# Keys and values as a paced list behind the queries, stored split weights for the filler, and another bank for the decode rows

## The chip, the core and the metric

The kernel runs on one core of a Trainium2 chip. Its time is the device time of one execution in microseconds; the median of three runs stands for a kernel. The engines are TensorE (PE; PEld is its weight load), VectorE (DVE), ScalarE (ACT), GpSimd (POOL) and SyncE (SP), which issues nearly all DMAs from one queue in program order.

## What is computed

One step of a hybrid decoder layer in fp32: 2048 prompt positions of width 1024, and 8 decode rows with 512 cached positions each in pages of 128.

```python
h = rms_norm(x, g)
q, k, v, fz, za, u, gv, zc = split(h @ w_in)        # 4 x 512, 8 heads, 4 x 512 columns
q, k = rms_norm(q, g_q), rms_norm(k, g_k)           # 8 heads of 64
c = cumsum(log_sigmoid(fz + b_f))                   # forget gates
s = q @ k.T * SCALE + c[t] - c[s]                   # causal
attn = softmax(s) @ v
mix = tril(w_s) @ rms_norm(gv) + b_s                # inside chunks of 128 positions
y = x + concat[attn * silu(za), u * mix * silu(zc)] @ w_out
```

The decode rows go through the same layer with keys, values and gates from the paged cache. The outputs are y, k, v and the log gates for both, and the normalised gv rows of the decode rows.

## The kernel before

**Precision.** Each fp32 matmul of the projections is made from three in a faster format: weights and inputs are split into a high and a low part (`wh`/`wl`, `hh`/`hl`), and hi x hi, lo x hi and hi x lo are added up in one PSUM bank.

**Stage one, 0 to about 590 us.** The input projection runs by units of columns `u`, in the order 3, 0, 1, 2 (tokens x columns of q, k, v and the gates), 4 (gv), 5, 6 (u and zc) and 7 (za). `load_unit` loads a unit's raw weights, scales and splits them, one unit ahead. At the end of each unit `sample_products` does the eight decode rows: 16 matmuls into a bank of the tag "acc", which the token products rotate through, too; ACT and DVE add its two halves (the tile `s`, L386 and L387). Keys and queries go to DRAM as `qk_hi` and `qk_lo`, values as `v_st`. Units 5 to 7 do only half of the prompt (`NCP` = 2 of 4 groups of 512 positions); the other half is left for the filler. Pages of cached keys (`kb`) are loaded and multiplied beside it in u=4 to 6.

**Stage two, about 590 to 1160 us.** Causal attention by units (h, c): a head and 512 query positions, c = 0 to 3, with 4c + 4 steps of 128 keys (`values`). One step is two score matmuls (`sc<-q,k`: the keys' high and low parts in `k1`, the high part and the rows of gates in `k2`), an exp on ACT (`p`), an accumulation on POOL (`acc`, L1014, for the denominators) and value matmuls (`av<-p,vst`) in groups. Before a unit its row maxima have to be known: `maxima` makes the scores transposed (`tp<-k,q`, needs only `k2`), reduces them on DVE (`mn`) and stores a row (`mrow`), which is one row of the queries' tile. The maxima run `AHEAD` of a head ahead of the values.

`load_queries` (L903 to L905) issues four DMAs: two of `qk_hi`, one of `qk_lo`, one of `mrow`. It is called `QLEAD` = 6 steps before a unit's end (at the first step of a unit of four) for the unit after. `load_keys` (`k2`, 512 KB, L860) is called at the start of a head's first unit for the next head, `load_values` (`k1` and `vst`, 1.5 MB) when the maxima of a head are through.

**The filler.** Between these steps the other half of units 5 to 7 (`fl<-hh,fh`) is issued, in a dose for each step (`FILL`; `FILL7` in the last three units). `fill_weights` loads 2 x 256 KB of raw weights, POOL scales them (L787), ACT casts the high part (L789), POOL subtracts for the low part (L790). When the filler is through it loads and splits the output weights (`load_out_weights`, `wo`), and then the first tiles of the output projection serve as filler in the last units. `gate` and `out_inputs` load what the products behind the attention need (`gz`, `ga`, `gr`; `g`, `xy`). Units run (0,0) to (5,3), then (6,0), (6,1), (6,2), (7,0), (6,3), (7,1), (7,2), (7,3).

**Stage three, from about 1140 us.** The output projection, `sc<-wo,am`.

**What sets the order.** TensorE's order is the order of the program. `Pe.clock` adds up estimated nanoseconds of matmuls; `later(ns, fn)` runs `fn` when that clock has gone on by ns, and so places DMAs and the work of other engines. On the chip each engine goes through its list in order and waits for what an instruction needs; a DMA that waits on SP holds up the DMAs behind it.

Of the kernel before, what the change touches and what calls it, by code (L numbers as in the profile page):

```python
# [9 lines left out]
F32 = mybir.dt.float32  # L10
F32R = mybir.dt.float32r
# [33 lines left out]
STLAST = 2500.0  # L45
SLAG = 3000.0
LAG = 6400.0
AVB = 8
# [5 lines left out]
UNITS = [(h, c) for h in range(6) for c in range(4)] + [(6, 0), (6, 1), (6, 2), (7, 0), (6, 3), (7, 1), (7, 2), (7, 3)]  # L54
AHEAD = 0.8
QLEAD = 6
PRE = 1.2
# [21 lines left out]
def hymba_step(ctx, tc, x_prompt, x_sample, cache_k, cache_v, cache_logf, page_table, g_norm, w_in,  # L79
# [39 lines left out]
    def s4(dt=F32, t="s4"):  # L119
        return med.tile([P, D], dt, tag="s4", name=tname(t))  # L120
# [26 lines left out]
    class Pe:  # L147

        clock = 0.0
        waiting = []  # L150
        given = 0
        decode, side, steps = 1e12, 1e12, None
        last = None
# [18 lines left out]
    def pump(all_=False):  # L172
        while Pe.waiting and (all_ or Pe.waiting[0][0] <= Pe.clock):
            give()
        if not all_ and Pe.clock >= Pe.side:
            m = next(mgen)
            mdone[0] += m
            Pe.side = Pe.clock + PACE if mdone[0] < AHEAD * MT else 1e12
        if not all_ and Pe.clock >= Pe.decode:
            Pe.decode = Pe.clock + (next(Pe.steps, None) or 1e12)  # L180

    def mm(out, lhsT, rhs, start, stop, ns):
# [84 lines left out]
    def log_sigmoid(out, z, rows, n, take):  # L267
# [20 lines left out]
        nc.vector.scalar_tensor_tensor(out, z, 0.0, c, op0=ALU.min, op1=ALU.subtract)  # L288

    def load_unit(segs, raws=None, between=None):  # L290

        n = sum(m for _, m in segs)
        out = []
        for k in range(KT):
            if k % 2 == 0:
                hi, lo = (s4(F32R, t)[:, :2 * n].rearrange("p (k f) -> p k f", k=2) for t in ("wh", "wl"))
            raw = (raws[k] if raws else raw2())[:, :n]
# [79 lines left out]

    def sample_products(unit, n, segs):
        po = bank("acc")
        for k in range(KT):  # L380
# [398 lines left out]

    def fill_weights(o, pair=None):  # L780
        hi, lo = (t.rearrange("p (k f) -> p k f", k=KT) for t in pair or (s4(F32R, "fh"), s4(F32R, "fl")))
        got = []

        def halves(half, raw):
            for k in range(4):
                kk = 4 * half + k
                nc.gpsimd.tensor_scalar(raw[:, k], raw[:, k], gT[:, kk:kk + 1], 0.0, op0=ALU.mult, op1=ALU.add)  # L787
            sl = slice(4 * half, 4 * half + 4)
            nc.scalar.copy(hi[:, sl], raw)  # L789
            nc.gpsimd.tensor_tensor(lo[:, sl], raw, hi[:, sl].bitcast(F32), op=ALU.subtract)  # L790
            got.extend((hi[:, k], lo[:, k]) for k in range(4 * half, 4 * half + 4))
        for half in range(2):
            raw = raw2().rearrange("p (k f) -> p k f", k=4)
            nc.sync.dma_start(raw, w[half * 512:(half + 1) * 512, o:o + P].rearrange("(k p) f -> p k f", p=P))
            later(FLAG * (1 + half), lambda half=half, raw=raw: halves(half, raw))
        return got
# [3 lines left out]
    def filler():  # L800
        jobs = [(o + f * P, f) for f in range(4) for o in (OZA, OU, OZC)] if NCP < 4 else []
        nxt = first.pop()
# [22 lines left out]
        for cp in range(NCP, 4):  # L825
            mx = s2(t="mxu")
            yield from u_steps(units[0], 0, f, cp, "fl", mx)
            yield 0
            yield from zc_steps(units[1], 0, f, cp, "fl", mx)
            if cp == 3:  # L830
                break
            yield 0
            while "k1" not in heads.get(NH - 1, {}):
                yield -1
            load_out_weights(0)
# [19 lines left out]

    def load_keys(h):

        k2 = s8(F32R, "k2")
        b = 512 + h * HD
        nc.sync.dma_start(k2[:HD].bitcast(F32), qk_hi[b:b + HD])  # L860
        nc.sync.dma_start(k2[HD:HD + 3].bitcast(F32), kx[h])
        return dict(h=h, k2=k2)

    def load_values(hd):

        k1 = s8(F32R, "k1")
        h = hd["h"]
        b = 512 + h * HD
        nc.sync.dma_start(k1[:HD].bitcast(F32), qk_hi[b:b + HD])
        nc.sync.dma_start(k1[HD:].bitcast(F32), qk_lo[b:b + HD])  # L870
        vst = s4(t="vst").rearrange("p (n e) -> p n e", e=HD)
        nc.sync.dma_start(vst, v_st[h])
        hd.update(k1=k1, vst=vst)

# [111 lines left out]
    def values(at):  # L986
# [3 lines left out]
        for kt in range(4 * c + 4):  # L990
            if kt == max(0, 4 * c + 4 - QLEAD) and at + 1 < len(UNITS):
                qload[UNITS[at + 1]] = load_queries(*UNITS[at + 1])
# [69 lines left out]
    def all_maxima():  # L1062
        for h in range(NH):
            yield from maxima(heads[h])
            if h + 1 < NH:
                load_values(heads[h + 1])

# [116 lines left out]
    with ExitStack() as p1:  # L1184
# [32 lines left out]
        for pos, u in enumerate(order):  # L1217
# [3 lines left out]
            if u <= 4:  # L1221
                for i in range(NT):
# [13 lines left out]
                    if i == NT - 2:  # L1236
                        group.insert(0, sample_products(unit, WID[u], SEGS[u]))
                    if u == 4 and i == KSTART:
# [6 lines left out]
                if u == 3:  # L1245
                    gates()
            else:
                for cp in range(NCP):
                    for f in range(2):
# [7 lines left out]
                        if cp == NCP - 1 and f == 1:  # L1257
                            group.insert(0, sample_products(unit, WID[u], SEGS[u]))
                        together(*group)
                    if u == 7 and cp == 0:  # L1260
                        heads[0] = load_keys(0)
                        load_values(heads[0])
                        fw = s8(F32R, "fw")
                        first.append(fill_weights(OZA, (fw[:, :D], fw[:, D:])))
                        Pe.side = Pe.clock + SSTART
# [83 lines left out]
```

## Time and profile before

| | |
|---|---|
| median of 3 runs | 1339.46 us (1339.31 to 1339.51) |
| profiled execution | 1342.54 us, span 1340.8 us, mean granted clock 0.989 |
| TensorE busy | 1297.8 us, 97% of the span |
| POOL busy | 622.2 us, 46% |
| DVE, ACT busy | 649.7 us (48%), 446.7 us (33%) |
| data moved by DMA | 182.56 MB, mean 136 GB/s |

The profile shows one execution. A row of the timeline gives start, duration, engine, line, operation, tile written and tiles read, and in brackets the idle time ahead of it on its engine with what ended it. The waits are given as engine, tile and line, what was waited for, and then the total in us, the number of waits and the longest. SPq is SP's queue of DMA issues.

### The profile page before, as it was taken

What the parts mean: (1) busy time and instruction counts of PE and PEld (TensorE: products, weight loads), DVE (VectorE), ACT (ScalarE), POOL (GpSimd) and SP (SyncE); (2) the same over time, 40 slices, a digit from 0 to 9 for tenths busy, and PEclk for the clock granted to TensorE, in tenths of its full rate; (3) what the DMA queues carried; (4) which work ended last, traced back from release to release, by engine and by line L of the source; (5) the groups of instructions that cost most, each with busy time, mean ns of one, the idle gap of its engine ahead of it and who ended that gap; (6) DMA issues with size and microseconds to landing.
All of it is one profiled execution on the core that took longest, in us unless ns stands there. A gap on an engine that the chain in (4) does not pass through costs nothing.

```text
span 1340.8 us, 19346 instructions
## 1 busy us (share of the span) xinstructions
PE 1297.8 (97%) x6544; PEld 1008.3 (75%) x6544; DVE 649.7 (48%) x1216; ACT 446.7 (33%) x805; POOL 622.2 (46%) x707
## 2 busy tenths in 40 slices
PE   6999999999999999999999999999999998999998
PEld 5999999999887777866666666656656664688877
DVE  4445654534677544264476353444355675322321
ACT  5542322222222110114454443534454456300100
POOL 3113343423223554416778666686768668600000
PEclk9999999999999999999999999999999998999999
DMA  6644353555213665635253845477374645573321
GB/s 218 188 120 111 87 142 111 156 144 152 60 42 102 178 182 146 178 88 134 64 130 107 198 120 142 133 189 180 87 195 117 179 126 198 156 238 121 102 80 47
DMA packets 170213, 182.56 MB, mean 136 GB/s; under 512 B 39106, under 2 KB 125442, under 8 KB 168554
## 3 DMA queue, kind: packets, MB, share of 16 engines
q1 hardware_dynamic: 166226, 172.55, 46.6%
q10 hardware_dynamic: 3488, 8.39, 1.6%
q8 instruction: 52, 0.85, 0.3%
q0 software_dynamic: 400, 0.38, 0.1%
q14 instruction: 47, 0.39, 0.1%
HBM read 121.14 MB, written 60.15 MB: 135 GB/s over the span
## 4 chain that ended last, share of the span: by engine, by line
PE 85%; DMA 5%; DVE 4%; issue 2%; SPq 1%; ACT 1%; POOL 1%; DVEq 0%; ACTq 0%; POOLq 0%
PE acc L183 35%; PE sc L183 22%; PE fl L183 10%; PE av L183 8%; PE tp L183 5%; PE tp L187 3%; DMA q<-qk_lo 1%; PE pm L183 1%; DMA xp<-in_x_prompt_dram 1%; DVE wl L265 1%; DMA vst<-v_st 1%; DVE mn L943 1%; DMA k<-qk_lo 1%; DVE wo L257 1%; DMA kb<-in_cache_k_dram 0%
## 5 line engine op out<-in xcount | busy, mean ns | idle before, releaser
L1014 POOL TENSOR_TENSOR acc<-acc,p 128x512 f32<-128x512 f32 (+3 forms) x256 | 285.9, 1117 | 60.4 <-ACT p L1005 47.3
L1005 ACT ACTIVATE p<-sc,zero 128x512 f32<-128x512 f32 (+1 forms) x320 | 194.7, 624 | 171.4 <-PE sc L183 163.6
L183 PE MATMUL acc<-wh,hh 128*128 128x384 f32 (+2 forms) x640 | 228.8, 358 | 0.0
L183 PE MATMUL acc<-wl,hh 128*128 128x384 f32 (+2 forms) x640 | 223.0, 348 | 0.6 <-DVE wl L265 0.6
L183 PE MATMUL acc<-wh,hl 128*128 128x384 f32 (+2 forms) x640 | 222.8, 348 | 0.6 <-DVE hl L257 0.6
L183 PE MATMUL sc<-q,k 128*128 128x512 f32 (+7 forms) x640 | 202.2, 396 | 9.7 <-ACT p L1005 2.9
L183 PE MATMUL sc<-wo,am 128*128 128x512 f32 x720 | 164.3, 390 | 0.0
L183 PEld LDWEIGHTS sc<-wo,am 128*128 128x128 f32 x720 | 134.9, 188 | 28.2
L945 DVE TENSOR_REDUCE mn<-tp 128x1 f32<-128x320 f32 (+5 forms) x192 | 118.6, 631 | 65.6 <-PE tp L183 64.4
L183 PEld LDWEIGHTS sc<-q,k 128*128 128x128 f32 (+1 forms) x640 | 119.1, 195 | 29.5 <-issue 7.3
L183 PE MATMUL av<-p,vst 128*64 128x512 f32 (+3 forms) x640 | 135.3, 543 | 0.0
L245 POOL TENSOR_SCALAR sm<-sm 128x6 f32<-128x6 f32 (+3 forms) x84 | 20.2, 241 | 238.4 <-DVE sm L398 171.1
L183 PE MATMUL tp<-k,q 66*128 66x384 f32 (+6 forms) x320 | 121.3, 394 | 7.9 <-DVE mn L943 3.4
L183 PEld LDWEIGHTS acc<-wh,hh 128*128 128x128 f32 x640 | 120.7, 189 | 7.2 <-ACT hh L252 0.2
L183 PEld LDWEIGHTS acc<-wl,hh 128*128 128x128 f32 x640 | 120.9, 189 | 5.9 <-DVE wl L265 1.5
L183 PEld LDWEIGHTS acc<-wh,hl 128*128 128x128 f32 x640 | 120.5, 188 | 6.3 <-DVE hl L257 1.2
L183 PEld LDWEIGHTS av<-p,vst 128*64 128x64 f32 x640 | 47.7, 137 | 67.5 <-issue 57.3
L943 DVE TENSOR_REDUCE mn<-tp 128x1 f32<-128x512 f32 (+7 forms) x128 | 66.9, 562 | 60.7 <-PE tp L183 60.6
L246 POOL TENSOR_TENSOR sm<-sm,mhalf 128x6 f32<-128x6 f32 (+3 forms) x84 | 89.6, 1067 | 6.7
L183 PEld LDWEIGHTS tp<-k,q 66*128 66x128 f32 x320 | 61.1, 192 | 34.0 <-DVE mn L943 6.6
L183 PE MATMUL acc<-hh,wh 128*128 128x512 f32 x192 | 76.2, 397 | 5.1 <-DVE s L387 5.1
L1138 DVE TENSOR_TENSOR xy<-xy,sc 128x512 f32<-128x512 f32 x30 | 20.6, 687 | 117.8 <-PE sc L183 117.8
(212 smaller groups left out, 1957.2 us busy)
## 6 DMA issues: line engine op xcount, KB each, us to landing
raw<-in_w_in_dram SPq DMA_DIRECT2D x40, 256.0 KB
kb<-in_cache_k_dram SPq DMA_DIRECT2D x32, 256.0 KB
k<-qk_hi SPq DMA_DIRECT2D x16, 512.0 KB
q<-qk_hi SPq DMA_DIRECT2D x64, 128.0 KB
vb<-in_cache_v_dram SPq DMA_DIRECT2D x32, 256.0 KB
g<-gm SPq DMA_DIRECT2D x16, 512.0 KB
xy<-in_x_prompt_dram SPq DMA_DIRECT2D x16, 512.0 KB
out_dram<-xy ACTq DMA_DIRECT2D x15, 512.0 KB
```

The costliest lines, as they stand in the source:

```text
L183: Pe.last = nc.tensor.matmul(out, lhsT, rhs, start=start, stop=stop).ins
L187: Pe.last = nc.tensor.transpose(out, in_, idn).ins
L245: nc.gpsimd.tensor_scalar(r, ss, inv_n, EPS, op0=ALU.mult, op1=ALU.add)
L246: nc.gpsimd.tensor_tensor(r, r, mhalf[:rows, :n], op=ALU.pow)
L257: nc.vector.tensor_tensor(lo, src, hi.bitcast(F32), op=ALU.subtract)
L265: nc.vector.scalar_tensor_tensor(lo, src, g, hi.bitcast(F32), op0=ALU.mult, op1=ALU.subtract)
L943: nc.vector.tensor_reduce(part[:, j_ % 4, n_:n_ + 1], sp, axis=AX.X, op=ALU.min)
L945: nc.vector.tensor_reduce(part[:, j % 4, n:n + 1], sp, axis=AX.X, op=ALU.min)
L1005: nc.scalar.activation(p[:, n0:], sp[:, n0:], AF.Exp, bias=zero1, scale=-1.0)
L1014: nc.gpsimd.tensor_tensor(acc[:, n0:], acc[:, n0:], p[:, n0:], op=ALU.add)
L1138: nc.vector.tensor_tensor(xy[:, fs], xy[:, fs], po, op=ALU.add)
```

## The change

- `load_head` replaces `load_keys` and `load_values`: it returns the loads of a head as a list, three pieces for `k2` and seven for `k1` and `vst`, of 256 KB each. The list is put up in the second step of a head's first unit for the next head, which is behind the query loads of that unit; one piece goes out 2500 ns of `Pe.clock` later and then one in 3000. Maxima and values issue what is left when they need it.
- Queries are issued ten steps before a unit's end instead of six if the next unit's maxima row is already stored, and else four steps before.
- `AHEAD` goes from 0.8 to 0.65 of a head, `FILL` from 0.50 to 0.46, with 0.9 in a head's first unit.
- `keep_unit` stores the split weights of units 5, 6 and 7 in DRAM (`ws`, 24 DMAs of 512 KB) 5 to 12.5 us after each of these units starts; `fill_weights` loads them from there, 24 DMAs of 512 KB in place of 24 of 256 KB, and POOL's 120 and ACT's 24 instructions at L787 to L790 are gone.
- The decode rows use a bank of the tag "pm" in all units but u=4.
- The filler waits for all of head 7's pieces before it loads output weights, where it waited for `k1`.

The numbers of TensorE's and DVE's instructions stay. The diff, cut:

```diff
-FILL = 0.50
+FILL = 0.46
+FILL0 = 0.9
-AHEAD = 0.8
-QLEAD = 6
+AHEAD = 0.65
+LSTEP = 3000.0
+LHEAD = 2500.0
+VPARTS = 7
+QLEAD = 10
...
     def pump(all_=False):
...
+        if not all_ and Pe.loads and Pe.clock >= Pe.load_at:
+            load_next()
...
+    def load_next():
+        Pe.loads.pop(0)()
+        Pe.load_at = Pe.clock + LSTEP
...
+    def keep_unit(u):
+        for j, pair in enumerate(list(split_)):
+            def store(j=j, pair=pair):
+                for r in range(2):
+                    nc.sync.dma_start(ws[u, :, r, 2 * j:2 * j + 2], pair[r].bitcast(F32))
+            later(KEEPLAG + j * KEEPSTEP, store)
...
-    def sample_products(unit, n, segs):
-        po = bank("acc")
+    def sample_products(unit, n, segs, tag):
+        po = bank(tag)
...
-    def fill_weights(o, pair=None):
+    def fill_weights(b, pair=None):
...
-                nc.gpsimd.tensor_scalar(raw[:, k], raw[:, k], gT[:, kk:kk + 1], 0.0, op0=ALU.mult, op1=ALU.add)
-            nc.scalar.copy(hi[:, sl], raw)
-            nc.gpsimd.tensor_tensor(lo[:, sl], raw, hi[:, sl].bitcast(F32), op=ALU.subtract)
...
-            nc.sync.dma_start(raw, w[half * 512:(half + 1) * 512, o:o + P].rearrange("(k p) f -> p k f", p=P))
+        for r, t in enumerate((hi, lo)):
+            nc.sync.dma_start(t.bitcast(F32), ws[b // 4, :, r, :, b % 4 * P:(b % 4 + 1) * P])
+        later(FLAG, lambda: got.extend((hi[:, k], lo[:, k]) for k in range(KT)))
...
+        return [lambda: keys(0), rows_of, lambda: keys(1)], [
+            lambda: both(0, 0), lambda: both(0, 1), lambda: vals(0),
+            lambda: both(1, 0), lambda: both(1, 1), lambda: vals(1), lambda: hd.update(all=True)]
...
         for kt in range(4 * c + 4):
-            if kt == max(0, 4 * c + 4 - QLEAD) and at + 1 < len(UNITS):
+            if kt == 1 and c == 0 and h < NH - 1:
+                Pe.loads += chain(*load_head(h + 1))
+                Pe.load_at = Pe.clock + LHEAD
+            if at + 1 < len(UNITS) and UNITS[at + 1] not in qload and kt >= 4 * c + 4 - (
+                    QLEAD if UNITS[at + 1] in shifted else 4):
                 qload[UNITS[at + 1]] = load_queries(*UNITS[at + 1])
...
         for h in range(NH):
+            while h not in heads or "k2" not in heads[h] or h and len(Pe.loads) > VPARTS:
...
+                load_next()
             yield from maxima(heads[h])
-            if h + 1 < NH:
-                load_values(heads[h + 1])
...
-                        group.insert(0, sample_products(unit, WID[u], SEGS[u]))
+                        group.insert(0, sample_products(unit, WID[u], SEGS[u], "acc" if u == 4 else "pm"))
...
     for at, (h, c) in enumerate(UNITS):
-        if c == 0 and h < NH - 1:
-            heads[h + 1] = load_keys(h + 1)
+        while "all" not in heads[h]:
+            load_next()
...
-        dose = FILL if at < len(UNITS) - 3 else FILL7
+        dose = FILL7 if at >= len(UNITS) - 3 else FILL0 if c == 0 else FILL
```

How the order on SP changes at three places. The first is around the queries for unit (2,1), which are loaded during (2,0). Before, `q_1059` was loaded behind raw filler weights and the 512 KB `k_1350` of the next head:

```order
645 L794 DMA raw_7636<-in_w_in_dram 128x4x128
646 L794 DMA raw_7638<-in_w_in_dram 128x4x128
647 L1045 DMA rT<-rows 4x128
648 L860 DMA k_1350_7653<-qk_hi 64x2048
649 L861 DMA k_1350_7653<-kx 3x2048
650 L903 DMA q_1059_6268<-qk_hi 64x512
651 L513 DMA mxu_7640<-mixT 128x512
652 L903 DMA q_1059_6268<-qk_hi 64x512
653 L904 DMA q_1059_6268<-qk_lo 64x512
654 L905 DMA q_1059_6268<-mrow 1x512
```

and with the change (here the tile is `q_1047`, and the key piece that follows is `k_1344`):

```order
678 L1076 DMA rT<-rows 4x128
679 L994 DMA mrow<-rows 4x128
680 L930 DMA q_1047_6242<-qk_hi 64x512 x2
681 L931 DMA q_1047_6242<-qk_lo 64x512
682 L932 DMA q_1047_6242<-mrow 1x512
683 L1127 DMA gz_7580<-zT 128x512
...
687 L811 DMA fh_7639<-ws 128x8x128
688 L811 DMA fl_7640<-ws 128x8x128
689 L539 DMA mxu_7643<-mixT 128x512
690 L1059 DMA aT<-at_7575 64x512
691 L883 DMA k_1344_7656<-qk_hi 64x1024
```

The filler weights and the key piece moved from in front of the queries to behind them.

The second place is SP around the queries for unit (3,3). Before, the gate inputs (`gz`, `ga`, `gr`) and the pages of cached values (`vb`) came after them:

```order
764 L1028 DMA aT<-at_8669 64x512
765 L528 DMA zT<-sz_8734 128x512
766 L903 DMA q_1059_6268<-qk_hi 64x512 x2
767 L904 DMA q_1059_6268<-qk_lo 64x512
768 L905 DMA q_1059_6268<-mrow 1x512
769 L1045 DMA rT<-rows 4x128
770 L1094 DMA gz_8832<-zT 128x512
771 L1095 DMA ga_8831<-aT 128x512
772 L1097 DMA gr_8833<-rT 64x512 x2
```

and with the change (the first and the last of four page loads are shown):

```order
803 L994 DMA mrow<-rows 4x128
804 L1127 DMA gz_8712<-zT 128x512
805 L1128 DMA ga_8711<-aT 128x512
806 L1130 DMA gr_8713<-rT 64x512 x2
807 L897 DMA vst_8726<-v_st 128x512
...
811 L677 DMA vb_8728<-in_cache_v_dram 128x512
...
823 L677 DMA vb_8728<-in_cache_v_dram 128x512
824 L930 DMA q_1047_6242<-qk_hi 64x512 x2
825 L931 DMA q_1047_6242<-qk_lo 64x512
826 L932 DMA q_1047_6242<-mrow 1x512
```

The queries moved behind the gate inputs, half of the values and four page loads.

The third place is SP around the queries of the last unit, (7,3). Before, two pairs of output-projection inputs stood between the query pieces:

```order
1037 L967 DMA mrow<-rows 4x128
1038 L903 DMA q_1059_6268<-qk_hi 64x512 x2
1039 L1115 DMA g_11551<-gm 128x1024
1040 L1116 DMA xy_11552<-in_x_prompt_dram 128x1024
1041 L1115 DMA g_11555<-gm 128x1024
1042 L1116 DMA xy_11556<-in_x_prompt_dram 128x1024
1043 L904 DMA q_1059_6268<-qk_lo 64x512
1044 L905 DMA q_1059_6268<-mrow 1x512
```

and with the change:

```order
1087 L1148 DMA g_11335<-gm 128x1024
1088 L1149 DMA xy_11336<-in_x_prompt_dram 128x1024
1089 L1059 DMA aT<-at_11380 64x512
1090 L1114 DMA raw_11391<-in_w_out_dram 128x512
1091 L994 DMA mrow<-rows 4x128
1092 L1076 DMA rT<-rows 4x128
1093 L930 DMA q_1047_6242<-qk_hi 64x512
1094 L1114 DMA raw_11397<-in_w_out_dram 128x512
1095 L930 DMA q_1047_6242<-qk_hi 64x512
1096 L931 DMA q_1047_6242<-qk_lo 64x512
1097 L932 DMA q_1047_6242<-mrow 1x512
```

The output-projection inputs moved ahead of all query pieces, and one load of output weights now stands between the pieces.

More of the change, by code (lines that the diff above doesn't have):

```diff
@@ L46 @@
 SLAG = 3000.0
+KEEPLAG = 5000.0
+KEEPSTEP = 2500.0
 LAG = 6400.0
@@ L151, in hymba_step @@
         given = 0
+        loads, load_at = [], 0.0
         decode, side, steps = 1e12, 1e12, None
@@ L235, in hymba_step @@
     rT = dr.tile([NH, SEQ], F32, name="rT")
+    ws = dr.tile([3, P, 2, KT, 4 * P], F32, name="ws")
     p_s = dr.tile([DB, D_IN], F32, name="p_s")
@@ L288, in log_sigmoid @@
         nc.vector.scalar_tensor_tensor(out, z, 0.0, c, op0=ALU.min, op1=ALU.subtract)
+    split_ = []
+    def keep_unit(u):
[4 more added lines that the diff above has]
+            later(KEEPLAG + j * KEEPSTEP, store)
     def load_unit(segs, raws=None, between=None):
@@ L293, in load_unit @@
         out = []
+        split_.clear()
         for k in range(KT):
@@ L296, in load_unit @@
                 hi, lo = (s4(F32R, t)[:, :2 * n].rearrange("p (k f) -> p k f", k=2) for t in ("wh", "wl"))
+                split_.append((hi, lo))
             raw = (raws[k] if raws else raw2())[:, :n]
@@ L777, in out_sample @@
         nc.sync.dma_start(ys, xys)
-    def fill_weights(o, pair=None):
+    def fill_weights(b, pair=None):
         hi, lo = (t.rearrange("p (k f) -> p k f", k=KT) for t in pair or (s4(F32R, "fh"), s4(F32R, "fl")))
         got = []
[L784 to L793, printed above, removed]
-            nc.sync.dma_start(raw, w[half * 512:(half + 1) * 512, o:o + P].rearrange("(k p) f -> p k f", p=P))
-            later(FLAG * (1 + half), lambda half=half, raw=raw: halves(half, raw))
+        for r, t in enumerate((hi, lo)):
+            nc.sync.dma_start(t.bitcast(F32), ws[b // 4, :, r, :, b % 4 * P:(b % 4 + 1) * P])
+        later(FLAG, lambda: got.extend((hi[:, k], lo[:, k]) for k in range(KT)))
         return got
@@ L800, in filler @@
     def filler():
-        jobs = [(o + f * P, f) for f in range(4) for o in (OZA, OU, OZC)] if NCP < 4 else []
+        jobs = [(b, f) for f in range(4) for b in (8 + f, 4 * (f // 2) + f % 2, 4 * (f // 2) + 2 + f % 2)]
         nxt = first.pop()
@@ L832, in filler @@
             yield 0
-            while "k1" not in heads.get(NH - 1, {}):
+            while "all" not in heads.get(NH - 1, {}):
                 yield -1
@@ L854, in fill, with load_head, keys, rows_of @@
             debt[0] -= got
-    def load_keys(h):
-        k2 = s8(F32R, "k2")
+    def load_head(h):
+        hd = heads[h] = dict(h=h)
         b = 512 + h * HD
[L860 to L873, printed above, removed]
+        def keys(a):
+            if a == 0:
+                hd["k2"] = s8(F32R, "k2")
+            cs = slice(a * 1024, (a + 1) * 1024)
+            nc.sync.dma_start(hd["k2"][:HD, cs].bitcast(F32), qk_hi[b:b + HD, cs])
+        def rows_of():
+            nc.sync.dma_start(hd["k2"][HD:HD + 3].bitcast(F32), kx[h])
+        def both(a, r):
+            if (a, r) == (0, 0):
+                hd["k1"] = s8(F32R, "k1")
+            cs = slice(a * 1024, (a + 1) * 1024)
+            nc.sync.dma_start(hd["k1"][r * HD:(r + 1) * HD, cs].bitcast(F32), (qk_lo if r else qk_hi)[b:b + HD, cs])
+        def vals(a):
+            if a == 0:
+                hd["vst"] = s4(t="vst").rearrange("p (n e) -> p n e", e=HD)
+            nc.sync.dma_start(hd["vst"][:, 8 * a:8 * a + 8], v_st[h, :, 8 * a:8 * a + 8])
+        return [lambda: keys(0), rows_of, lambda: keys(1)], [
+            lambda: both(0, 0), lambda: both(0, 1), lambda: vals(0),
+            lambda: both(1, 0), lambda: both(1, 1), lambda: vals(1), lambda: hd.update(all=True)]
     def pieces(nk):
@@ L1063, in all_maxima @@
         for h in range(NH):
+            while h not in heads or "k2" not in heads[h] or h and len(Pe.loads) > VPARTS:
+                if not Pe.loads:
+                    raise RuntimeError(h)
+                load_next()
             yield from maxima(heads[h])
-            if h + 1 < NH:
-                load_values(heads[h + 1])
     wo_hl = {}
@@ L1247, in hymba_step @@
             else:
+                keep_unit(u - 5)
                 for cp in range(NCP):
@@ L1257, in hymba_step @@
                         if cp == NCP - 1 and f == 1:
-                            group.insert(0, sample_products(unit, WID[u], SEGS[u]))
+                            group.insert(0, sample_products(unit, WID[u], SEGS[u], "acc" if u == 4 else "pm"))
                         together(*group)
                     if u == 7 and cp == 0:
-                        heads[0] = load_keys(0)
-                        load_values(heads[0])
+                        for piece in chain(*load_head(0)):
+                            piece()
                         fw = s8(F32R, "fw")
-                        first.append(fill_weights(OZA, (fw[:, :D], fw[:, D:])))
+                        first.append(fill_weights(8, (fw[:, :D], fw[:, D:])))
                         Pe.side = Pe.clock + SSTART
```

## The prediction

> **What bounds the kernel now.** I read the page first, then who waited for whom on TensorE, then ten-microsecond windows around the waits, then the timelines there.
>
> ```profile
> span 1340.8 us, 19346 instructions
> PE 1297.8 (97%) x6544; PEld 1008.3 (75%) x6544; DVE 649.7 (48%) x1216; ACT 446.7 (33%) x805; POOL 622.2 (46%) x707
> ```
>
> TensorE (PE) is busy for 1297.8 of 1340.8 us. The change issues as many matmuls as before, of the same shapes, so at most 43 us is to be had from its idle time, and beside that what the granted clock costs. The waits of TensorE (total, times, longest):
>
> ```profile
> PE acc L183 <- DVE s L387: 5.1, 3, 2.8
> PE tp L183 <- DVE mn L943: 3.4, 6, 1.2
> PE sc L183 <- ACT p L1005: 2.9, 3, 1.8
> PE sc L183 <- DMA q<-qk_hi: 2.4, 1, 2.4
> PE sc L183 <- DMA q<-qk_lo: 2.3, 1, 2.3
> PE sc L183 <- issue: 1.9, 1, 1.9
> PE fl L183 <- DVE sz L499: 1.8, 2, 1.4
> ```
>
> Windows (PE, PEld, DVE, ACT, POOL busy; granted clock; DMA share; GB/s):
>
> ```profile
> 490.00:500.00 10.00, 9.76 (x43) 8.10 (x44) 4.24 (x7) 2.14 (x3) 7.25 (x7) 1.00 0.72 209
> 750.00:760.00 10.00, 7.51 (x30) 5.14 (x27) 3.79 (x8) 2.68 (x6) 4.32 (x8) 0.83 1.00 215
> 900.00:910.00 10.00, 8.06 (x35) 5.59 (x34) 4.12 (x10) 2.95 (x6) 4.21 (x5) 0.83 1.04 232
> 1110.00:1120.00 10.00, 7.51 (x39) 4.00 (x38) 9.16 (x7) 6.98 (x15) 9.69 (x8) 1.00 0.38 119
> 1120.00:1130.00 10.00, 9.39 (x27) 3.96 (x27) 3.05 (x5) 5.38 (x10) 9.45 (x9) 0.66 0.42 113
> 1130.00:1140.00 10.00, 7.67 (x37) 5.02 (x36) 3.91 (x5) 6.88 (x12) 5.81 (x6) 0.90 1.02 377
> ```
>
> At 750 and 900 the clock is 0.83 over ten microseconds: 10 x 0.17 = 1.7 us of work lost after the wait, beside the wait. The timelines show which waits these are. Entering unit (2,1), the queries were issued behind a 512 KB key load:
>
> ```profile
> 743.46 0.45 SPq L860 DMA_DIRECT2D k<-qk_hi  x1
> 744.52 0.45 SPq L903 DMA_DIRECT2D q<-qk_hi  x1
> 747.35 0.45 SPq L904 DMA_DIRECT2D q<-qk_lo  x1
> 754.45 1.08 PE L183 MATMUL sc<-q,k 128*128 128x512 f32 x2 [2.38 <-DMA q<-qk_hi]
> ```
>
> Entering (4,1) they stood behind four page loads and the key load. The wait is named "issue"; but the last query piece (L905) went out only 3.8 us before the matmul that needs it, and I take it for the same wait. Two us later a 128x512 matmul takes 0.63 us; at the full clock it is 0.40, as in the row at 437.65 further down:
>
> ```profile
> 890.11 3.94 SPq L651 DMA_DIRECT2D vb<-in_cache_v_dram  x4
> 900.75 0.44 SPq L905 DMA_DIRECT2D q<-mrow  x1
> 904.51 0.82 PE L183 MATMUL sc<-q,k 128*128 128x512 f32 x2 [1.94 <-issue]
> 906.59 0.63 PE L183 MATMUL fl<-hh,fh 128*128 128x512 f32 x1
> ```
>
> Entering the last unit, (7,3), 2 MB of out-projection inputs were issued between the two parts of the queries:
>
> ```profile
> 1123.94 2.33 SPq L903 DMA_DIRECT2D q<-qk_hi  x2
> 1127.22 0.33 SPq L1115 DMA_DIRECT2D g<-gm  x1
> 1129.02 0.51 SPq L904 DMA_DIRECT2D q<-qk_lo  x1
> 1134.10 0.48 PE L183 MATMUL sc<-q,k 128*128 128x512 f32 x1
> 1136.91 2.56 PE L183 MATMUL sc<-q,k 67*128 67x512 f32 x7 [2.33 <-DMA q<-qk_lo]
> ```
>
> **The change part by part.** The sum is made against the profiled execution, 1342.54 us around its span of 1340.8; it lies 3.1 us (0.23%) above the median of 1339.46, and I take the 3.1 off at the end.
>
> *Decode rows in another bank: -2.3.* The waits on L387 are 5.1 us in three. The longest ends the stage u=4, which keeps its bank:
>
> ```profile
> 437.07 0.50 PE L183 MATMUL acc<-hh,wh 128*128 128x512 f32 x1 [2.79 <-DVE s L387]
> 437.65 0.40 PE L183 MATMUL acc<-hh,wl 128*128 128x512 f32 x1
> 490.24 0.50 PE L183 MATMUL acc<-hh,wh 128*128 128x512 f32 x1 [1.73 <-DVE s L387]
> ```
>
> The "pm" bank is otherwise used only in u=4, so nothing waits for it in u=5 and u=6: 5.1 - 2.8 = 2.3 go, 1.73 of them in the row at 490. Neither window lost clock (490 to 500: 1.00). Bounds -2.3 to 0, if the next accumulator is no earlier free.
>
> *Queries ahead of the keys, entering (2,1): -4.1.* By the order of SP nothing large now stands in front of them; the first key piece is issued after them. 2.38 of waiting and 1.7 of clock; bounds -4.1 to 0.
>
> *Entering (4,1): -3.0.* The key load is gone from in front, but the four page loads stay, and four gate inputs (768 KB) are now ahead of all query pieces, where they stood between them. The queries are issued a little earlier (QLEAD 10 instead of 6 steps, cut to the unit's length). Of 1.94 + 1.7 = 3.6 I take 3.0, nearer to the full gain because 512 KB less are ahead; bounds -3.6 to 0.
>
> *Queries whose lead falls: +6.* Where the row of maxima is not stored yet, the queries now wait until four steps before the unit's end, six before. Six steps measured 10.2 us (1123.94 to 1134.10), so four are an estimated 6.8 us. In front of (1,3) now stand 1.8 MB (both filler weights, 512 KB each, and three pieces of 256 KB), in front of (3,3) 2.05 MB (gate inputs, half the values, four page loads). At the 215 to 232 GB/s of the windows with a full DMA, those and the 384 KB of the queries themselves take 9.7 and 11 us: 2.9 and 4.2 us too long if all is issued at once, nothing if it is issued earlier. Bounds 0 to 2.9 + 4.2 + 2 x 1.7 = 10.5. I take two us for each, and the clock slice in a little over half the cases: 2 x (2 + 1) = 6.
>
> *Entering (7,3): -1.5.* The 2 MB of g and xy are now issued some 12 us before the queries, but the lead falls to four steps and 256 KB of output weights stand between the query pieces. Of 2.33 + 1.7 = 4.0 I take 1.5; bounds -4.0 to +1.5 (the wait one clock slice longer).
>
> *Filler doses and maxima: -1.* POOL is the bound from 1094 on: 9.69 and 9.45 of 10 us busy, one accumulation after the other:
>
> ```profile
> 1095.10 3.65 PE L183 MATMUL av<-p,vst 128*64 128x512 f32 x16
> 1100.57 9.47 POOL L1014 TENSOR_TENSOR acc<-acc,p 128x512 f32<-128x512 f32 x8 [0.79 <-ACT p L1005]
> ```
>
> 9.47 / 8 = 1.18 us for each, while a step without filler needs two score matmuls and two value matmuls of TensorE at 3.65 / 16 = 0.23 us each, 0.9 us. By the order of TensorE the filler now reaches through (6,3), but the out products enter (7,3) after the ninth step instead of the fourth, so about as many steps stand bare as before. TensorE lost 2.5 us idle in 1110 to 1120. Bounds -3 to +3; I take -1, as by my count of the order a few steps fewer are bare.
>
> *Filler weights loaded, not made: -1.* What goes from POOL and ACT:
>
> ```profile
> L787 POOL TENSOR_SCALAR raw<-raw,gT 128x128 f32<-128x128 f32 x96 | 35.6, 389 | 5.0 <-DMA raw<-in_w_in_dram 5.0
> L790 POOL TENSOR_TENSOR fl<-raw,fh 128x512 fp32r<-128x512 f32 x22 | 28.2, 1283 | 7.2 <-ACT fh L789 7.0
> ```
>
> 64 us of POOL and 24 casts of ACT lie beside TensorE's work, so they are worth at most the waits that their crowding causes: those on mn and sz, 3.4 + 1.8 = 5.2. Bounds -5.2 to 0; I take 1. The new loads wait on SP until TensorE has left their buffer, and the queue stands behind them; that is in the +6.
>
> *Storing the weights: +1.* 24 stores of 512 KB go out in u=5, 6 and 7, 4.2 MB each time within some 10 us.
>
> ```profile
> q1 hardware_dynamic: 166226, 172.55, 46.6%
> q10 hardware_dynamic: 3488, 8.39, 1.6%
> 490.00:540.00 50.00, 49.15 (x214) 39.03 (x215) 23.00 (x32) 6.92 (x10) 28.94 (x26) 1.00 0.63 182
> 540.00:590.00 50.00, 49.19 (x224) 38.55 (x223) 14.87 (x27) 7.50 (x13) 12.29 (x17) 1.00 0.39 106
> POOL kb L668 <- DMA kb<-in_cache_k_dram: 24.4, 15, 6.3
> ```
>
> The queue moves 172.55 MB in 46.6% of the span, 276 GB/s, or 391 in q10's large rows: 11 to 15 us of all DMA engines per stage of 50 us that is 39 to 63% busy. It fits over a stage and not in its moment: a load issued behind it comes up to 15 us late. POOL already waits up to 6.3 us for the pages of keys without a wait of TensorE, so I take 1. Bounds 0 to 13.5 (below).
>
> Sum: -2.3 - 4.1 - 3.0 + 6 - 1.5 - 1 - 1 + 1 = -5.9. 1342.5 - 5.9 = 1336.6, less 3.1: 1333.5 us.
>
> [...]
>
> **The rivals.**
>
> *A, the queries are late elsewhere.* (1,3) and (3,3) cost their bound of 10.5 instead of 6, and (7,3) keeps its wait: -5.9 + 4.5 + 1.5 = +0.1, 1339.6 us. For it speaks that page loads take 3.94 us of SP's time for four; against it that much of the 2 MB is issued well before the queries.
>
> *B, the stores take over (slower).* If the 15 us of backlog exceed the lead of the loads of pages and mixing inputs, the DVE and ACT queues stop behind them and TensorE runs out of accumulators. It decides when a load is over some 12 us late (one group of accumulators, estimated from the 50 us of a stage in four groups). Price, as at 437: 2.8 + 1.7 = 4.5 in each of three stages, 13.5 instead of the 1 in the sum: 1333.5 + 12.5 = 1346.0. Against it: POOL's 6.3 us wait did no harm.
>
> *C, no new waits.* The 6 falls to 0 and (7,3) yields all 4.0: -5.9 - 6 - 2.5 = -14.4, 1325.0 us. For it: the loads ahead wait for their own buffers and may be out early.
>
> *D, the queries are as late as before* in (2,1) and (4,1), since other loads fill the place of the keys: -5.9 + 7.1 = +1.2, 1340.7. The order shows no such load before (2,1).
>
> **How the numbers follow.** A measurement of this kernel can tell 0.2%, 2.7 us, from no change: faster is below 1336.8, slower above 1342.1. Forecast 0.45 (1330 to 1337; nearly all faster), C 0.13 (faster), A 0.19 and D 0.06 (nearly all within 0.2%), B 0.17 (slower). Faster 0.57, same 0.24, slower 0.19. The range reaches from C to the middle of B: 1324 to 1345.
>
> **What would show it.** Right: no wait on s at 490 and 538, none entering (2,1), clock 1.00 there; a wait of one to five us on q entering (1,3) or (3,3); POOL some 64 us less busy. Wrong: waits on s or mxu around 500 to 590 (B); q waits in (2,1) (D); a longer bare stretch in (7,2) and (7,3), where POOL's accumulations set the pace and a later out projection costs more than the 3 allowed; or the first filler weights late at 590, behind their own stores.

## The result, and the profile after

The changed kernel took 1326.85 us (median of 5 runs, 1325.52 to 1332.61), the kernel before 1339.46 (1336.08 to 1339.87): a ratio of 0.991 (95% interval 0.989 to 0.994). A second measurement on another chip, beside six runs of it, gave 1328.54 us and 0.991 (0.989 to 0.993). Forecast were 1333.5 us and a ratio of 0.996. The gain is twice the forecast's. The time lies inside the range of 1324 to 1345 and outside the forecast's own band of 1330 to 1337; it is close to the rival C, which had a chance of 0.13.

The page of the profile after has this ahead:

```profile
span 1325.0 us, 19322 instructions
PE 1289.8 (97%) x6544; PEld 1005.7 (76%) x6544; DVE 646.6 (49%) x1216; ACT 432.1 (33%) x781; POOL 559.0 (42%) x587
```

POOL is 63 us less busy, as the removed instructions had it. The waits of TensorE (helper and lines have moved: L196 is the matmul, L413 the sum of the decode rows, L1067 the reciprocal of the denominators, L983 the row maxima):

```profile
PE tp L200 <- DVE sm L1067: 4.1, 3, 2.0
PE tp L200 <- DVE mx L983: 2.4, 1, 2.4
PE acc L196 <- DVE s L413: 2.4, 1, 2.4
PE sc L196 <- DMA q<-qk_hi: 1.5, 1, 1.5
PE fl L196 <- DVE sz L525: 1.5, 1, 1.5
PE tp L200 <- DVE mn L970: 1.5, 1, 1.5
PE tp L196 <- DVE mx L983: 1.1, 1, 1.1
PE sc L196 <- ACT p L1036: 0.7, 2, 0.4
```

Two of the three waits on s are gone, the three waits on queries are gone, and exp holds TensorE up for 0.7 us instead of 2.9. New are the waits on mx and most of those on sm (1.3 us before): small transposes whose DVE work is late. The one wait on queries that is left is a new one, 1.5 us entering the very first unit, (0,0). The windows at the places of the prediction, and at two of the new waits (columns as before):

```profile
490.00:500.00 10.00, 10.00 (x46) 8.29 (x45) 2.94 (x6) 1.41 (x2) 5.61 (x6) 1.00 1.04 366
690.00:700.00 10.00, 9.57 (x35) 6.77 (x37) 4.40 (x12) 4.78 (x9) 4.00 (x4) 0.66 0.36 100
740.00:760.00 20.00, 20.00 (x106) 13.64 (x104) 10.41 (x17) 9.26 (x17) 11.04 (x12) 1.00 0.82 225
880.00:900.00 20.00, 20.00 (x106) 12.78 (x106) 9.37 (x17) 8.24 (x16) 10.42 (x11) 1.00 0.56 162
1120.00:1130.00 10.00, 9.37 (x33) 5.03 (x33) 6.50 (x8) 6.64 (x12) 9.69 (x8) 0.83 0.60 160
```

Around the entries to (2,1) and (4,1), 740 to 760 and 880 to 900, TensorE is busy throughout at the full clock, where 1.9 to 2.5 us of ten were idle and the clock was 0.83. At 490 the stores fill the DMA engines (share 1.04, 366 GB/s) and TensorE does not notice. At 690 a wait of 2.40 us on mx costs the clock (0.66).

The account of the two profiled executions: the span fell by 15.8 us. Idle stretches of TensorE over 0.1 us after its first instruction went from 28.7 to 21.1 us. The trace's record of the clock has it at half for 3.41 us at a time (called a slice below), inside the program eight times before and six times after. From that clock I count each slice as half of its length, 1.7 us, an estimate (in the slice at 437.7 of the changed kernel a 128x512 matmul starts every 0.43 us, just ahead of it every 0.24), so two fewer are worth 3.4. That leaves 4.8 us which no wait of such a length shows; where they went stays open. The profiled execution before lies 3.1 us above its median and the one after on it, so that the medians differ by 12.6 only.

### The profile page after: what moved, and what is told of

Same layout as the page of the kernel before. It is cut to its first block, busy times and chain, and to the rows that moved or that the text cites. A ratio compares the mean times of both kernels' runs of the same rounds, so it can differ in the third digit from the quotient of the medians.

```text
span 1325.0 us, 19322 instructions
## 1 busy us (share of the span) xinstructions
PE 1289.8 (97%) x6544; PEld 1005.7 (76%) x6544; DVE 646.6 (49%) x1216; ACT 432.1 (33%) x781; POOL 559.0 (42%) x587
## 4 chain that ended last, share of the span: by engine, by line
PE 90%; DVE 3%; DMA 2%; issue 2%; ACT 1%; POOL 1%; SPq 1%; DVEq 0%; POOLq 0%; ACTq 0%
PE acc L196 36%; PE sc L196 22%; PE fl L196 10%; PE av L196 9%; PE tp L196 6%; PE tp L200 4%; PE pm L196 3%; DMA xp<-in_x_prompt_dram 1%; DMA q<-qk_hi 1%; POOL acc L1045 0%; DMA g<-gm 0%; ACT p L1036 0%; SPq L326 0%; DVE wl L279 0%; DVE mn L972 0%
## 5 line engine op out<-in xcount | busy, mean ns | idle before, releaser
L196 PE MATMUL acc<-wh,hh 128*128 128x384 f32 (+2 forms) x640 | 229.0, 358 | 0.0
L196 PE MATMUL acc<-wl,hh 128*128 128x384 f32 (+2 forms) x640 | 223.3, 349 | 1.2 <-DVE wl L279 1.2
L196 PE MATMUL acc<-wh,hl 128*128 128x384 f32 (+2 forms) x640 | 223.0, 348 | 0.6 <-DVE hl L271 0.6
L196 PE MATMUL sc<-q,k 128*128 128x512 f32 (+7 forms) x640 | 202.4, 397 | 2.2 <-DMA q<-qk_hi 1.5
L196 PE MATMUL sc<-wo,am 128*128 128x512 f32 x720 | 164.1, 390 | 0.0
L196 PEld LDWEIGHTS sc<-wo,am 128*128 128x128 f32 x720 | 135.0, 188 | 28.2
L196 PE MATMUL av<-p,vst 128*64 128x512 f32 (+3 forms) x640 | 135.0, 542 | 0.0
L196 PEld LDWEIGHTS sc<-q,k 128*128 128x128 f32 (+1 forms) x640 | 119.1, 197 | 18.8 <-ACT p L1036 3.6
L196 PEld LDWEIGHTS acc<-wh,hh 128*128 128x128 f32 x640 | 120.8, 189 | 7.0 <-ACT hh L266 0.2
L196 PEld LDWEIGHTS acc<-wl,hh 128*128 128x128 f32 x640 | 121.0, 189 | 6.8 <-DVE wl L279 2.3
L196 PEld LDWEIGHTS acc<-wh,hl 128*128 128x128 f32 x640 | 120.5, 188 | 6.2 <-DVE hl L271 1.1
L196 PE MATMUL tp<-k,q 66*128 66x384 f32 (+6 forms) x320 | 121.4, 393 | 3.3 <-DVE mx L983 1.1
L196 PEld LDWEIGHTS av<-p,vst 128*64 128x64 f32 x640 | 47.8, 137 | 67.0 <-issue 58.3
L1043 POOL TENSOR_TENSOR acc<-p 128x512 f32<-128x512 f32 x32 | 41.6, 1300 | 104.7 <-ACT p L1036 91.6
L196 PEld LDWEIGHTS tp<-k,q 66*128 66x128 f32 x320 | 61.1, 192 | 29.8 <-issue 5.9
```

The source lines that it names most:

```text
L196: Pe.last = nc.tensor.matmul(out, lhsT, rhs, start=start, stop=stop).ins
L1043: nc.gpsimd.tensor_tensor(acc, p0, p, op=ALU.add)
```

## The experiments

Each kernel was timed in five rounds against the kernel before on its chip. The ratio is to that kernel; the changed kernel's is 0.991. The first four ran on one chip, the next four on a second, then three on a third and c_tp on a fourth, so across these groups the ratios are compared, not the medians.

| label | what it is | median us | ratio, 95% interval |
|---|---|---|---|
| u_bank | decode rows in "acc" again | 1331.85 | 0.993 (0.990 to 0.995) |
| u_stored | filler weights made, not loaded | 1329.18 | 0.991 (0.988 to 0.994) |
| u_keys | k2 ahead of the queries again | 1328.64 | 0.990 (0.987 to 0.994) |
| u_doses | old doses, maxima 0.8 ahead | 1347.38 | 1.005 (1.002 to 1.007) |
| after_again | the changed kernel | 1328.54 | 0.991 (0.989 to 0.993) |
| u_ahead | maxima 0.8 ahead, new doses | 1353.14 | 1.009 (1.007 to 1.011) |
| u_fill | old doses, maxima 0.65 ahead | 1330.27 | 0.992 (0.989 to 0.994) |
| only_fill | the kernel before, new doses | 1338.04 | 0.998 (0.996 to 0.999) |
| only_list | the kernel before, list and 0.65 | 1336.01 | 0.996 (0.994 to 0.997) |
| lead2 | two steps of lead instead of four | 1328.17 | 0.990 (0.987 to 0.992) |
| c_both | further edits, below | 1335.51 | 0.996 (0.995 to 0.998) |
| c_tp | one further edit, below | 1324.82 | 0.989 (0.986 to 0.991) |

My theory at first (T) was that each part gives what its own waits had cost, and that the queries carry most. Four kernels undid one part each.

**u_bank.**

```diff
-sample_products(unit, WID[u], SEGS[u], "acc" if u == 4 else "pm")
+sample_products(unit, WID[u], SEGS[u], "acc")
```

> The changed kernel with the decode rows' products in the tag acc in every unit again. Theory T (each part gives what its own waits cost before): 2.3 to 2.7 us slower than the changed kernel, about 1329.5 us, the waits on s at 488 and 538 are back at 1.7 and 0.6 us, nothing else moves. Rival: the bank only shifts the wait to the next accumulator, within 1 us of the changed kernel.

The median came to 1331.85 us; the interval overlaps that of the changed kernel, so the rival's "within 1 us" is not excluded by the time. The waits are back as they were before, here in the view of waits of this kernel:

```profile
PE acc L196 <- DVE s L413: 5.1, 3, 2.2
```

The step of the bank holds by the trace. Its size is not told apart from the spread of the runs.

**u_stored.** `fill_weights` as before, no `keep_unit`.

```diff
-                keep_unit(u - 5)
-        for r, t in enumerate((hi, lo)):
-            nc.sync.dma_start(t.bitcast(F32), ws[b // 4, :, r, :, b % 4 * P:(b % 4 + 1) * P])
+            (raw loads, POOL's scaling, ACT's cast, POOL's subtraction)
```

> The changed kernel with the filler's weights loaded raw and split by POOL and ACT as before, nothing stored. Theory T (the gain is in the query loads): within 2 us of the changed kernel, POOL some 64 us busier, TensorE's waits on DVE hardly longer. Rival R (relief of POOL, ACT and DVE carries the part of the gain that the queries do not): 4 us or more slower, about 1331 us or above, with more or longer waits of TensorE on mn, mx, sm and sz.

No difference: 0.991 for both. The page has POOL's time back,

```profile
PE 1290.9 (97%) x6544; PEld 1006.2 (76%) x6544; DVE 659.9 (50%) x1216; ACT 445.2 (34%) x805; POOL 622.8 (47%) x707
```

and TensorE's busy time hardly moved (1289.8). So 64 us of POOL, 13 of ACT and 18.9 MB of added traffic are worth nothing measurable here, together: rival R fell on the time. The trace has one half of what R named: the waits on mn are longer, 5.3 us against 2.2. Against that, the wait of 1.5 us entering (0,0) is gone, so two effects seem to cancel (more on it below).

**u_keys.**

```diff
+        if c == 0 and h < NH - 1:
+            Pe.loads += chain(*load_head(h + 1))
+            for _ in range(3):
+                load_next()
```

(at the start of a unit; the list is no longer put up in its second step)

> The changed kernel with the three pieces of the next head's k2 issued at the start of a head's first unit, ahead of the queries of its second unit, as before; the other pieces stay paced. Theory T (the key load in front made the queries late): waits on q of 1 to 2.4 us come back entering some of the units (h,1), with half-clock slices, 4 to 8 us slower than the changed kernel. Rival: it was the raw weights and page loads in front, not the keys: no wait on q entering (h,1), within 1.5 us.

No wait came back, and the time is that of the changed kernel. Theory T fell here, and what the rival expected came. In the timelines of SP and TensorE of this kernel, entering (2,1), the key pieces stand in front of the queries just as before the change, and the matmul does not wait:

```profile
740.82 0.45 SPq L883 DMA_DIRECT2D k<-qk_hi  x1
742.36 0.54 SPq L930 DMA_DIRECT2D q<-qk_hi  x1
746.51 0.44 SPq L932 DMA_DIRECT2D q<-mrow  x1
747.80 1.50 PE L196 MATMUL av<-p,vst 128*64 128x512 f32 x8
749.24 0.50 PE L196 MATMUL fl<-hh,fh 128*128 128x512 f32 x1
751.41 0.62 PE L196 MATMUL sc<-q,k 128*128 128x512 f32 x2
```

Between the last value matmuls and the first score matmul now lie nine matmuls of filler, 749.24 to 751.41; before there was one group of three and a wait of 2.38. So moving the keys behind the queries was not the only remedy.

**u_doses.**

```diff
-FILL = 0.46
-FILL0 = 0.9
-AHEAD = 0.65
+FILL = 0.50
+FILL0 = 0.50
+AHEAD = 0.8
```

> The changed kernel with the old doses of filler (0.50 in every unit but the last three) and the maxima 0.8 of a head ahead. Theory T: within 2 us of the changed kernel, either way; what is gained or lost is where POOL sets the pace, about 1090 to 1140. Rival D (the doses carry the rest of the gain, since steps are better covered): 3 us or more slower, idle of TensorE on exp between 1100 and 1125 back at 3 us.

Rival D's "3 us or more slower" came, but not its reason, since no wait on exp came back. The kernel is slower than even the one before, by 0.5%. Its new waits are on `k<-kx` (3.3, 2.8 and 0.7 us), the rows of gates in `k2`, at the first maxima of a head. (Its profiled execution, 1340.20 us, is one of its fastest.) So I split the two settings, with theory A (the 0.65 is what the list needs) against rival F (the dose is what counts).

**u_ahead, u_fill and only_fill.** Each undoes or does one half of the diff above: u_ahead has only AHEAD = 0.8, u_fill only the two doses; only_fill is the kernel before with FILL = 0.46 and 0.9 in a head's first unit.

> The changed kernel as it is, beside the variants on one chip. Both theories: a ratio of about 0.991 to the kernel before.

> The changed kernel with the maxima 0.8 of a head ahead again, the new doses kept. Theory A (with the keys put up behind the queries, maxima that run 0.8 ahead need the next head's k2 in its first units, before the list has brought it): waits of TensorE on the rows of gates of k2 (k<-kx) at the start of heads come back, some 7 to 10 us with their half-clock slices, so nearly all of the loss of the kernel with both settings undone. Rival F (the doses of filler are what counts): within 3 us of the changed kernel, no wait on kx.

> The changed kernel with the old dose of filler, 0.50 in a head's first unit too, the maxima 0.65 ahead kept. Theory A: within 3 us of the changed kernel, no wait on k2. Rival F: the 0.9 in a head's first unit, some nine filler matmuls or 2 us between the queries' loads and their use, is what made the queries land in time: waits on q of 1 to 2.4 us come back entering some (h,1), 4 us or more slower.

> The kernel before with the new doses of filler alone (0.46, and 0.9 in a head's first unit); keys, weights, bank and the maxima's 0.8 as before. Rival F: the waits on q entering (2,1) and (4,1) go, 1.9 and 2.4 us with their clock slices, 5 us or more faster than before. Theory A (the parts need each other): within 3 us of the kernel before.

Theory A held for u_ahead, and the loss was more than it said: 24.6 us over the changed kernel on the same chip. In the waits, the timeline and a window of u_ahead:

```profile
PE tp L196 <- DMA k<-kx: 8.8, 2, 6.9
PE tp L196 <- issue: 8.6, 3, 5.3
974.71 0.61 SPq L883 DMA_DIRECT2D k<-qk_hi  x1
976.54 3.73 SPq L677 DMA_DIRECT2D vb<-in_cache_v_dram  x4
982.15 0.47 SPq L932 DMA_DIRECT2D q<-mrow  x1
982.67 0.26 SPq L886 DMA_DIRECT2D k<-kx  x1
985.51 0.45 PE L196 MATMUL tp<-k,q 66*128 66x128 f32 x1 [6.88 <-DMA k<-kx]
980.00:990.00 10.00, 4.49 (x13) 3.64 (x14) 0.62 (x2) 0.69 (x1) 1.26 (x1) 0.55 0.79 213
```

The first maxima of head 6 need the three rows of gates, 24 KB together; they are the second piece of the list, which is not 256 KB like the others. With 0.8 of a head the maxima are due so early that the rest of k2 is pulled from the list at once; it goes onto SP behind four page loads and the next queries, at 982.67, and TensorE stands for 6.88 us and runs at half the clock from 981 to 991. The waits named "issue" stand at the same instruction of other heads; at 757.93 and 1057.44 the rows were issued 3.8 and 3.4 us before, and I take them for the same wait. In the profiles the loss adds up: against after_again 15.0 us more of idle TensorE and six more slices (10.2 us) make 25.2 of the 25.9 us between the spans.

In the changed kernel, with 0.65, no wait on kx shows. But the 0.65 alone does not do it: u_fill and only_list, which have 0.65 and the old doses, wait on kx once, at head 6:

```profile
PE tp L196 <- DMA k<-kx: 2.2, 1, 2.2
970.50 0.34 SPq L886 DMA_DIRECT2D k<-kx  x1
974.11 0.45 PE L196 MATMUL tp<-k,q 66*128 66x128 f32 x1 [2.25 <-DMA k<-kx]
```

(from u_fill). With the maxima at 0.8, then, the changed kernel is slower than the one before; the maxima have to start later, and the new doses take away the last wait. A kernel before with 0.65 and nothing else was not run, so what the 0.65 does without the list is not shown.

The interval of u_fill overlaps that of the changed kernel, and no wait stands entering (2,1) or (4,1); rival F's claim on it fell, and so did theory A's "no wait on k2". But only_fill shows that the dose alone can do this, too: its waits entering (2,1) and (4,1) are gone. (The other dose also shifts loads: on its SP the raw weights come behind the queries of (2,1), at 746.12.) It is 0.2% faster than before, 3.7 us, between what the two theories said. Its profile shows its slowest execution (1343.07 us), in which queries came late at another place (2.16 us at 987, with a clock of 0.57 in the 20 us behind it, and 3.13 entering (7,3)). Either the list with the rule for the queries and the 0.65, or the dose, cures the two entries; which of the first three does it no run separates.

**only_list.** The kernel before with the list, the rule for the queries and the 0.65, which is the diff of the change without its bank, stored weights and doses.

> The kernel before with the list of key and value pieces, the new rule for the queries and the maxima 0.65 of a head ahead; bank, filler weights and doses of filler as before. Theory L (the list and the 0.65 belong together and carry the gain, the other parts little): 8 to 11 us faster than before, no wait on q entering (2,1), (4,1) or (7,3), waits on s at 488 and 538 as before. Rival: the gain is spread over parts that only the whole has: 5 us faster or less.

It is 0.4% faster, 5.1 us: some 40% of the change's gain. All three waits on queries are gone, but others stand in their place (view of waits of this kernel):

```profile
PE tp L200 <- DVE sm L1076: 7.7, 4, 4.3
PE acc L196 <- DVE s L413: 5.3, 3, 2.8
PE tp L196 <- DMA k<-kx: 2.1, 1, 2.1
```

The whole has 4.1, 2.4 and 0 there. The bank and the doses each remove some of this in the traces (u_bank, u_fill), and undoing one of the other parts never moves the median clearly: the gain is spread, as the rival had it.

**lead2.**

```diff
-                    QLEAD if UNITS[at + 1] in shifted else 4):
+                    QLEAD if UNITS[at + 1] in shifted else 2):
```

> The changed kernel with the queries of units whose maxima row is late issued two steps before the unit's end instead of four. Theory Q (SP spreads the loads ahead over several us by its own issue time, so nothing is queued when the queries go out, and they land some 2 us after the last issue): waits on q entering (1,3) and (3,3) stay under 1.5 us each, 0 to 3 us slower. Rival, the prediction's step (1.8 to 2.05 MB ahead at 220 GB/s): with 3.4 us less of lead, waits of 4 us and more entering (1,3) and (3,3), 8 us or more slower.

No wait entering (1,3) or (3,3), and no slower. But the experiment changed less than it meant to: the last query piece for (3,3) was issued at 851.8, 4.1 us before the unit, as in the changed kernel (851.88, 4.1), since the same loads stand ahead of it on SP and follow one another until then. So it does not show what a shorter lead costs; it shows that the rule does not set the moment of issue there.

**c_both and c_tp.** What was left were waits on late DVE work.

```diff
-"acc" if u == 4 else "pm"
+"tp" if u == 4 else "pm"
-SLAG = 3000.0
+SLAG = 4500.0
-                        later(2000, done)
+                        later(4000, done)
```

c_tp has only the first of these edits.

> The changed kernel with three further edits: the decode rows of u=4 in the tag tp, the transposes of the denominators 4000 ns of the clock after their sums instead of 2000, those of the maxima 4500 instead of 3000. Theory W (what is left are waits of TensorE on late DVE work, and each costs a clock slice beside it): the wait on s at 434 goes (2.4 and 1.7 us), those on sm and mx at 688, 1074 and 1118 fall under 0.5 us (some 6 us and up to 6.8 of clock): 6 to 14 us faster than the changed kernel. Rival: POOL and DVE are behind there anyway and the wait moves to the next instruction that needs them, within 3 us; or the later rows of maxima make the queries late and it is slower.

> The changed kernel with one further edit: the decode rows of u=4 in a bank of the tag tp, which the token products do not use. Theory W: the wait on s at 434 (2.4 to 2.7 us) and its clock slice (1.7) go, and nothing behind it changes order: 4 us faster than the changed kernel, a ratio of about 0.988 to the kernel before. Rival: what stage one gains, the attention gives back, since POOL sets its pace: within 1.5 us of the changed kernel.

In c_both the waits on s and on mx are gone and the one on sm (L1067) as well, and unit (2,1) starts at 742.0 instead of 748.9. It is slower than the changed kernel nevertheless, by 7 us. Other waits took their place: TensorE waits on maxima (mn) and, near the end, on exp:

```profile
PE sc L196 <- ACT p L1036: 6.4, 3, 2.5
PE tp L196 <- DVE mn L972: 3.8, 4, 2.2
1087.96 0.62 ACT L266 CAST wo<-raw 128x512 fp32r<-128x512 f32 x1 [2.57 <-DMA raw<-in_w_out_dram]
1125.40 0.62 ACT L266 CAST wo<-raw 128x512 fp32r<-128x512 f32 x1 [2.01 <-DMA raw<-in_w_out_dram]
1126.04 1.27 ACT L1036 ACTIVATE p<-sc,zero 128x512 f32<-128x512 f32 x2
```

In its list ACT has casts of output weights in front of these exps, and stands at them until the weights have landed; the wait of TensorE that ends at 1126.78 is this one. So it is not POOL that holds exp up there. Which of the two later transposes moved the loads and casts is not shown.

c_tp keeps the lags. The wait at 434 is gone, with its slice of half clock, and the median of 1324.82 us is the lowest measured; against the changed kernel's 0.991 its 0.989 is 0.25% or some 3.4 us less, near the 4 of theory W. The intervals overlap, so the rival's "within 1.5 us" is not excluded.

## Why the prediction was right, and which of its steps were not

The change made the kernel faster, as forecast, and most of the waits that the prediction named are gone. The size came out right only within the wide range; the forecast was 6.7 us too slow, about as much as the one term that put a price on the queries.

- *The bank, -2.3.* Right in the trace: 5.1 us in three waits became 2.4 in one, so -2.7.
- *Entering (2,1) and (4,1), -4.1 and -3.0.* Both waits and both losses of clock are gone, -4.1 and -3.6. The reason was half right at most. The key load in front of the queries was there, but u_keys and only_fill have it, too, and do not wait; entering (4,1), u_keys even has the four page loads, the gate inputs and the keys ahead of the queries. u_doses has 1 MB of filler weights ahead of the queries of (2,1), without the keys, and does not wait there. It fits these runs that the lateness was a sum of what stood in front and how little TensorE had left to do; the change acts on both, and no run varies one of them alone.
- *Queries whose lead falls, +6.* This term was mis-sized: it measured 0, and the wait of one to five us entering (1,3) or (3,3), which the prediction named as a sign that it is right, did not come. It assumed that 2 MB are issued at once and the queries wait behind them. The timeline of SP in the changed kernel, the entry to (3,3), and two windows, of the changed kernel and of the one before:

```profile
842.79 0.35 SPq L1127 DMA_DIRECT2D gz<-zT  x1
844.79 0.58 SPq L897 DMA_DIRECT2D vst<-v_st  x1
846.36 3.70 SPq L677 DMA_DIRECT2D vb<-in_cache_v_dram  x4
850.10 1.09 SPq L930 DMA_DIRECT2D q<-qk_hi  x2
851.88 0.47 SPq L932 DMA_DIRECT2D q<-mrow  x1
856.00 0.63 PE L196 MATMUL sc<-q,k 128*128 128x512 f32 x2
842.79:850.10 7.31, 7.31 (x36) 3.71 (x34) 0.73 (x2) 1.62 (x3) 4.15 (x4) 1.00 0.81 243
900.75:904.50 3.75, 1.82 (x11) 0.80 (x8) 0.68 (x1) 0.58 (x1) 1.49 (x3) 1.00 1.10 268
```

  The loads ahead go out over 7.3 us, in which 243 GB/s, 1.8 MB, were moved. So most of the 2 MB had moved by 850.1, and a last piece 4.1 us ahead of its unit was early enough. Entering (1,3), 2.9 us were. Before, 3.8 us had not been enough at (4,1): there the DMA engines were full all that time (1.10). From this I take it that the price of bytes ahead is what is still queued at the issue, not what was issued before; no experiment varied it alone (lead2 did not). With 0 in place of 6 the sum is -11.9 and the time 1327.5, near the measured 1326.9.
- *Entering (7,3), -1.5.* The wait on queries is gone, 2.33 us and its slice. A wait of 1.99 us on sm stands in the same place with a clock of 0.83 behind it (window at 1120): the place gained some 0.3 us instead of 1.5.
- *Doses and maxima, -1.* At the end exp cost 0.7 us instead of 2.9, and the two slices of half clock behind its longest wait are gone: some -5.6 together, beyond the bounds of -3 to +3. It was not the doses: only_fill, which has them alone, waits 2.3 us on exp, and only_list, without them, 0.6. What the step missed is that the 0.65 is no matter of cover. The list needs it: u_ahead, without it, loses 24.6 us. The prediction had no term for k2 coming late.
- *Weights loaded, not made, -1, and stored, +1.* Together 0 by u_stored. The stores filled the DMA engines at 490 (1.04) without a wait; rival B did not come. The loads did have a price, at a place for which the prediction's sum has no term. The first filler weights, now 1 MB instead of 512 KB, go out ahead of the queries of (0,0):

```profile
587.14 0.38 SPq L811 DMA_DIRECT2D fh<-ws  x1
587.62 0.66 SPq L811 DMA_DIRECT2D fl<-ws  x1
591.28 0.60 SPq L931 DMA_DIRECT2D q<-qk_lo  x1
596.41 0.47 PE L196 MATMUL sc<-q,k 128*128 128x512 f32 x1 [1.50 <-DMA q<-qk_hi]
587.14:596.40 9.26, 7.58 (x33) 4.89 (x32) 7.22 (x15) 0.00 (x0) 0.00 (x0) 1.00 1.00 252
```

  Eight of the ten profiles of kernels that load these weights have a wait here, 0.5 to 2.9 us, and none of the four of kernels that make them. With the DMA engines full all the time (1.00), this looks like what the +6 had in mind, entering another unit.
- *New waits.* The prediction had none on sm and mx; they are 7.6 us (1.3 before) and four slices of half clock in the changed kernel (windows at 690, 0.66, and at 1120, 0.83, for three of them). Whether the kernel would be as much faster without them is not shown: c_both takes most of them away and is slower.

That the sum of the steps with 0 for the queries comes within a microsecond of the measurement is in part luck, as errors of both signs cancel, and does not show each step: some 4.8 us of the two profiles' difference are in no wait over 0.1 us, and the parts are not additive (only_list and only_fill give 5.1 and 3.7 us, and undoing the list's order or the doses costs nothing measurable).

## What to carry to other kernels

Before pricing a load by the bytes issued ahead of it, look at when they were issued: here, entering (3,3), SP took 0.35 to 0.93 us for one load, 2 MB went out over 7.3 us, and most of it had moved when the queries followed; where 1 MB was issued within 1.2 us, some 2 us ahead of the queries, they came late in eight of ten profiles. A paced list of loads has to be matched with the first use of what it brings; here 0.15 of a head more of lead for the maxima turned a gain of 0.9% into a loss of 0.9%. Where a late operand has two remedies, loads moved back or work moved in front of the use, undo each by itself before believing either.

## What the runs showed of the hardware

In these profiles some waits shorter than one clock slice cost the clock, and some did not. In the changed kernel a wait of 1.46 us on mn at 716 is followed by 3.41 us at half clock, and one of 1.46 us on sz at 963 is not. In its clock record the slices begin on a grid of 3.413 us: 690.3, 717.6, 1076.0 and 1120.4 lie 74, 82, 187 and 200 such lengths behind 437.7. So waits of one length can fall differently on it: in the changed kernel the 1.46 us on mn lie inside one stretch of the grid (714.2 to 717.6) and those on sz are cut at 963.35 into 0.18 and 1.28 us; in lead2, where the grid cuts the wait of 1.46 us on mn into 1.17 and 0.29 us, no slice follows either. I laid the grid over the fourteen profiles, from 20 to 1310 us, and counted how long TensorE was idle in each stretch that ran at the full clock. All 43 stretches with 1.9 us or more of idle time were followed by a slice, 31 of 71 with 1.0 to 1.9, one of 92 with 0.5 to 1.0, and none of the 4962 with less; in the profiles of before and after alone it was 7 of 7, 5 of 11, none of 12 and none of 710. How many slices follow is open: behind the wait at 987 in only_fill there are five, with TensorE hardly idle in them (busy for 17.84 of the 20 us from 987 on at a clock of 0.57, and 2.16 of these 20 us are the wait). In the changed kernel waits of 1.46 to 2.40 us were enough for a slice (those that end at 436.3, 690.4, 717.4, 1075.4 and 1120.3).

The grid fits a part of the spread of 7 us between runs of the changed kernel. The runs without a profile do not show their slices but list a mean granted clock: it is 0.995 in the fastest and 0.988 in the slowest run, but 0.992 both at 1326.85 and at 1330.58 us, so something else differs, too.
